# Layer B of a hybrid encoder: two contraction steps per token tile, and four query blocks' scores in one piece

## The chip, the cores and the metric

The kernel runs on one core of one Trainium2 chip. The metric is device time in microseconds (us) of one execution, as the median of the runs; lower is better. The core's engines are TensorE (PE in the profile; PEld is its loading of weights), VectorE (DVE), ScalarE (ACT), GpSimd (POOL) and SyncE (SP), which issues most of the DMAs.

## The reference

The reference is a two-layer bidirectional encoder block on 512 tokens of 1024 values in float32: per layer an RMS norm, one combined input projection, a token mixer, a SiLU gate and an output projection with a residual add. Layer A (dilated windows) is not changed. Layer B is a neighbourhood attention on an 8 x 64 grid of tokens with 16 heads of 64:

```python
def mixer_b(hn, w_in, w_out, q_gain, k_gain, rpb):
    proj = hn @ w_in                                  # 1024 -> 4 * 1024
    q, k, v, gate = jnp.split(proj, 4, axis=-1)
    q = rms_norm(q.reshape(b, s, N_HEADS, HEAD_DIM), q_gain) * (HEAD_DIM ** -0.5)
    k = rms_norm(k.reshape(b, s, N_HEADS, HEAD_DIM), k_gain)
    v = v.reshape(b, s, N_HEADS, HEAD_DIM)
    ...
        logits = jnp.einsum('bhcqd,bhrcjd->bhcqrj', qr, kr).astype(jnp.float32) + bias
        logits = jnp.where(col_valid[:, :, None, :], logits, NEG_INF)
        p = jax.nn.softmax(logits.reshape(b, N_HEADS, n_cb, NA_COL_BLOCK, wr * NA_SLAB), axis=-1)
        ...
        out = jnp.einsum('bhcqrj,bhrcjd->bhcqd', p, vr)
    ...
    y = y * jax.nn.silu(gate)
    return y @ w_out
```

## The kernel before, in words

**Precision.** Every large product is made of three matmuls: each operand is split into a high part (`h`, float32r) and a low rest (`l`), and `mm3` adds high x high, high x low and low x high into one accumulator. Weights arrive by DMA as `wraw` (8 buffers); ScalarE casts them to `wh` (6 buffers), and VectorE or GpSimd subtracts to get `wl` (5 buffers; in layer B two of five on GpSimd). The generator `splits` does this some steps ahead of use, and `next(wsteps)` hands out the next step's pair.

**Layer B.** The 16 heads are handled in 8 turns of two heads each (`hc`, called a head below, counted from 0). In `main_b`, `project_qk` makes queries, keys and values (384 columns) for four tiles of 128 tokens: the tokens' activations `hn_h`, `hn_l` are the stationary operand, the weights are streamed. `project` loops over the 8 steps of the contraction (`KT`), and in each step over the four tiles, with three matmuls each. It has one accumulator (`acc`, 512 float32 per partition) for each tile, and the pool `ps_acc` has four. After the last step `evac` copies each tile with ScalarE into `raw` (`rawq`, `rawk` or `rawb` in the profile). Then `project_t` makes the gate (512 columns, 24 matmuls) in one accumulator of the same pool, which VectorE reads into `gt`. The next head's projection follows.

**The side work.** While `main` runs, `run` pumps a second generator, `side`, between any two groups of three matmuls. In it `side_b` transposes queries and keys of the head just projected (`tp`), splits them (`qh`, `ql`, `kh`, `kl`) and computes scores, softmax and weighting. A number that `side` yields is a delay on a modelled clock that counts matmul columns; a tuple waits for a stamp; a `guard` that `main` yields makes `side` run until that stamp is there. `scores(u)` makes the logits of two of the four query blocks for both heads (`log`, two banks of the pool `ps_side`, which has four): 12 matmuls on 64 rows each, in pairs that run side by side. `softmax` follows per head and pair of blocks: a VectorE reduction that adds the bias and takes the row's minimum (into a small tile `mn`, of which there are four), a ScalarE exponential, a VectorE reciprocal, a ScalarE scaling. Then the probabilities `p` are transposed: by VectorE and a DMA round trip in heads 0 to 5, by TensorE (`turn_p`) in heads 6 and 7. `weigh` multiplies them with the values (`o`), later.

**Order.** TensorE's order is the order of the program (`manual_schedule`). The other engines' order is planned by a scheduler; `keep_in_program_order` pins single instructions behind what was written before on that engine. `chore` drops one piece of the gate's SiLU (VectorE) at a time into the loop of `project`. Every engine instruction issued through the helper class has line 85 in the profile, matmuls have line 324 and transposes 328, so groups are told apart by their tiles.

Of the kernel before, what the change touches and what calls it, by code (L numbers as in the profile page):

```python
# [27 lines left out]
KT = 8  # L28
# [18 lines left out]
def tile_hybrid_encoder(  # L47
# [24 lines left out]
    held = [False]  # L72
# [26 lines left out]
    def sb(t, off, dims):  # L99
        return bass.AP(t.tensor, t.offset + off, [t.ap[0]] + dims)  # L100
# [13 lines left out]
    def bank(name):  # L114

        return ps_side.tile([P, 512], F32, tag="side", name=name)
# [194 lines left out]
    def steps():  # L311
        for h, l, n in splits():
            for c in range(0, h.shape[1], n):
                yield h[:, c : c + n], l[:, c : c + n]
# [5 lines left out]
    def matmul(o, l, r, share=1, **kw):  # L320

        cols = max(r.free_size() / 2.4, l.free_size() / 1.2)
        clock[0] += (cols if r.dtype == F32R else r.free_size() * 4 / 2.4 * l.free_size() / P) / share
        nc.tensor.matmul(o, l, r, **kw)  # L324
# [5 lines left out]
    def mm3(o, lh, ll, rh, rl, first, last, **kw):  # L330
        matmul(o, lh, rh, start=first, stop=False, **kw)
        matmul(o, lh, rl, start=False, stop=False, **kw)
        matmul(o, ll, rh, start=False, stop=last, **kw)

    def mm3_heads(os, lh, ll, rh, rl, last):

        for n, (l, r) in enumerate(((lh, rh), (lh, rl), (ll, rh))):
            for hd in range(2):
                hs = slice(64 * hd, 64 * hd + 64)
                matmul(os[hd], l(hs), r(hs), share=2, start=(n == 0), stop=(last and n == 2))  # L340
# [14 lines left out]
    def chore(now):  # L355

        if now and chores and next(chores[0], "end") == "end":
            chores.pop(0)
# [18 lines left out]
    def project(stat_h, stat_l, n, evac, guard, need=None, after=None):  # L377

        acc = {i: ps_acc.tile([P, 512], F32, tag="acc", name="acc") for i in range(4)}
        for k in range(KT):  # L380
            chore(1 <= k < KT - 2)
            if need:
                yield need, min(k + 1, KT - 1)
            if k == KT - 1:
                yield guard
            h, l = next(wsteps)
            for i in range(4):
                mm3(acc[i][:, :n], stat_h(k, i), stat_l(k, i), h, l, k == 0, k == KT - 1)
                if k == KT - 1:
                    evac(i, acc[i])  # L390
                yield
            if after:
                yield "xn", k
                after(k)

    def project_t(acc):

# [89 lines left out]
    wsteps = steps()  # L487
    wsteps = chain([next(wsteps)], wsteps)
# [128 lines left out]
    def project_qk(n, ns, key, hc, guard, first=False, **kw):  # L617

        box = []

        def evac(i, acc):
            if not box:
                box.append(raw_q() if key == "rawq" else part(0) if key == "rawk" else raw_b(hc, n))
                box.append(sums())
                held[0] = held[0] or (key == "rawk" and hc == 0)
            raw, ss = box
            dst, src = raw[:, i, :], acc[:, :n]
            if first:
                act.copy(dst, src)
                return  # L630
            act.activation(dst, src, AF.Copy, scale=rs_n[:, i : i + 1])
            (squares_soon if key != "raw" else squares)(raw[:, i, : ns * 64], ss, i, ns, key != "raw")

        tile_of = lambda hn: lambda k, i: hn[:, k, P * i : P * (i + 1)]
        yield from project(tile_of(hn_h), tile_of(hn_l), n, evac, guard, **kw)
        raw, ss = box
        if first:
            st["first"] = raw, ss
            stamp["first",] = clock[0]
            return  # L640
        normed(raw, ss, ns, key, hc)
# [196 lines left out]
    def normalise(pr, mn):  # L838

        vec.reciprocal(mn[:, 3:4], mn[:, 2:3])  # L840
        act.activation(pr, pr, AF.Copy, scale=mn[:, 3:4])
# [428 lines left out]
    def side_b(hc):  # L1270
# [28 lines left out]

        at = lambda a, hd, i: 448 * a + 224 * hd + 32 * i  # L1300

        def scores(u):
            lgs = [bank("log") for _ in range(2)]
            for b in (2 * u, 2 * u + 1):
                if b < 3:
                    m = lambda t_, hs: t_[hs, P * b : P * b + 256]
                else:
                    m = lambda t_, hs: sb(t_[hs], 0, [[384, 2], [1, P]])
                qs = slice(P * b, P * b + P)
                o = 256 * (b % 2)  # L1310
                mm3_heads(
                    [lg[:, o : o + 256] for lg in lgs],
                    lambda hs: qh[hs, qs], lambda hs: ql[hs, qs], lambda hs: m(kh, hs), lambda hs: m(kl, hs), True,
                )
            return [(hd, u, softmax(hd, u, lgs[hd])) for hd in range(2)]

        def softmax(hd, u, lg):
            pr = wk.tile([P, 512], F32, tag="p", name="p", bufs=PB)
            for b in (2 * u, 2 * u + 1):
                mn = wk.tile([P, 4], F32, tag="mn", name="mn", bufs=4)  # L1320
                o = 256 * (b % 2)
                if b < 3:
                    parts = ((slice(0, P), o),)
                    n, ec = 256, 0
                else:
                    parts = ((slice(0, 64), o), (slice(64, P), o + P))
                    n, ec = 128, 256
                for rows, c in parts:
                    vec.tensor_tensor_reduce(
                        out=pr[rows, o : o + n],  # L1330
                        in0=lg[rows, c : c + n],
                        in1=e[rows, hd, ec : ec + n],
                        scale=1.0,
                        scalar=3.0e38,
                        op0=ALU.add,
                        op1=ALU.min,
                        accum_out=mn[rows, 0:1],
                    )
                act.activation(
                    pr[:, o : o + n], pr[:, o : o + n], AF.Exp, bias=mn[:, 0:1], scale=-1.0, accum_out=mn[:, 2:3]  # L1340
                )
                normalise(pr[:, o : o + n], mn)
            return pr
# [29 lines left out]
                pass  # L1373
            return o

        held = []
        for u in range(2):
            held += scores(u)
            yield 1200 if u == 0 else 2400
        if far(hc):  # L1380
            turned = turner(448)
            turners.append(turned)
# [25 lines left out]
    def side():  # L1408
# [33 lines left out]
        for hc in range(NHC):  # L1442
            yield from side_b(hc)
# [94 lines left out]
```

## Time and profile before

| | |
|---|---|
| Time, median of 3 runs | 845.55 us (844.61 to 847.19) |
| Profiled execution, span from first to last instruction | 844.7 us; the page gives no other time of it |
| TensorE busy | 829.5 us (98%), 6611 matmuls |
| VectorE, ScalarE, GpSimd busy | 631.8, 508.2, 291.7 us |
| Granted TensorE clock, mean | 0.999 |
| DMA | 131.97 MB, mean 156 GB/s |

How to read it: TensorE's instructions are pipelined, so a record begins before the one before has ended, and its busy share is close to full also where it works below its peak. A row of the timeline gives start, duration, engine, line, operation, output and inputs by the program's names, shape and count; in brackets stands how long the engine stood idle before it and who released it. A row of the waits gives the total in us, the number of times and the longest.

### The profile page before, as it was taken

The page shows a single profiled execution, that of the slowest core. Times are in us where ns is not written, and L with a number is a line of the kernel's source. Part 1 is how long each engine was busy: PE and PEld are TensorE (multiplying, and loading weights), DVE is VectorE, ACT ScalarE, POOL GpSimd, SP SyncE. Part 2 cuts the span into 40 slices and gives each one's busy share as a digit, 9 for nine tenths or more (in the row PEclk, how much of TensorE's full clock was granted, in tenths as well). Part 3 has the DMA queues.
Part 4 walks back from the last instruction along what each step waited for, and adds up shares of the span by engine and source line. Part 5 has one row for each costly group of instructions (what it writes and reads, how often), then busy time and mean ns, then how long its engine had stood idle before and what let it go on. Part 6 is the DMA issues. An engine that isn't in the chain of part 4 may idle for free.

```text
span 844.7 us, 18126 instructions
## 1 busy us (share of the span) xinstructions
PE 829.5 (98%) x6611; PEld 686.0 (81%) x6611; DVE 631.8 (75%) x1653; ACT 508.2 (60%) x1066; POOL 291.7 (35%) x259
## 2 busy tenths in 40 slices
PE   9999999999999999999999999999999999999998
PEld 7877878878877878878877887789998898889786
DVE  7898997896995886896896876566668767776742
ACT  7656766846846846747747728554546664666440
POOL 5042343543533533533532514213123222322201
PEclk9999999999999999999999999999999999999999
DMA  9426766676676785785776554473265456644212
GB/s 342 141 57 170 190 155 151 141 172 195 133 172 201 158 194 167 159 205 132 162 177 167 119 186 144 150 237 111 93 192 161 132 146 180 173 135 115 85 51 100
DMA packets 56169, 131.97 MB, mean 156 GB/s; under 512 B 7184, under 2 KB 24528, under 8 KB 55952
## 3 DMA queue, kind: packets, MB, share of 16 engines
q1 hardware_dynamic: 49456, 108.39, 41.7%
q0 software_dynamic: 6048, 22.02, 15.3%
q8 instruction: 52, 0.85, 0.4%
q10 hardware_dynamic: 576, 0.41, 0.2%
q14 instruction: 37, 0.30, 0.1%
HBM read 111.73 MB, written 11.72 MB: 146 GB/s over the span
## 4 chain that ended last, share of the span: by engine, by line
PE 77%; ACT 8%; DVE 7%; DMA 4%; issue 2%; POOL 1%; SPq 0%; ACTq 0%; DVEq 0%; POOLq 0%
PE acc L324 64%; PE log L324 5%; PE o L324 4%; ACT p L85 4%; PE tp L328 3%; DMA wraw<-in_w 2%; ACT wh L85 1%; DVE wl L85 1%; DVE na L85 1%; DMA yr<-y_d 1%; ACT rawk L85 1%; DVE rawq L85 1%; DVE gt L85 1%; POOL sq L85 1%; DVE tr L85 1%
## 5 line engine op out<-in xcount | busy, mean ns | idle before, releaser
L85 POOL TENSOR_TENSOR wl<-wraw,wh 128x512 fp32r<-128x512 f32 (+1 forms) x153 | 198.5, 1298 | 434.8 <-PE acc L324 214.4
L85 ACT CAST wh<-wraw 128x512 fp32r<-128x512 f32 (+1 forms) x360 | 209.5, 593 | 194.7 <-PE acc L324 155.0
L85 DVE TENSOR_TENSOR wl<-wraw,wh 128x512 fp32r<-128x512 f32 (+1 forms) x207 | 159.3, 773 | 45.5 <-PE acc L324 33.3
L324 PE MATMUL acc<-wh,hn_h 128*128 128x384 f32 (+1 forms) x488 | 186.4, 382 | 2.7 <-DVE gt L85 1.5
L324 PE MATMUL acc<-wl,hn_h 128*128 128x384 f32 (+1 forms) x488 | 177.6, 364 | 1.7 <-DVE wl L85 1.7
L324 PE MATMUL acc<-wh,hn_l 128*128 128x384 f32 (+1 forms) x488 | 177.4, 364 | 0.0
L85 ACT ACTIVATE p<-p,mn 128x256 f32<-128x256 f32 (+2 forms) x248 | 137.7, 585 | 32.3 <-DVE mn L85 32.3
L324 PEld LDWEIGHTS acc<-wh,hn_h 128*128 128x128 f32 x488 | 92.1, 189 | 21.3 <-issue 6.8
L324 PEld LDWEIGHTS acc<-wl,hn_h 128*128 128x128 f32 x488 | 92.3, 189 | 10.0 <-DVE wl L85 2.6
L324 PEld LDWEIGHTS acc<-wh,hn_l 128*128 128x128 f32 x488 | 92.0, 189 | 9.8
L324 PE MATMUL acc<-wh,mix_h 128*128 128x512 f32 x224 | 89.1, 398 | 0.0
L324 PE MATMUL acc<-wl,mix_h 128*128 128x512 f32 x224 | 87.5, 390 | 0.0
L324 PE MATMUL acc<-wh,mix_l 128*128 128x512 f32 x224 | 87.4, 390 | 0.0
L324 PE MATMUL acc<-hn_h,wh 128*128 128x512 f32 x192 | 79.0, 412 | 0.3 <-ACT rawb L85 0.2
L324 PE MATMUL acc<-hn_h,wl 128*128 128x512 f32 x192 | 75.1, 391 | 0.0
L324 PE MATMUL acc<-hn_l,wh 128*128 128x512 f32 x192 | 75.0, 391 | 0.0
L85 DVE STREAM_TRANSPOSE pt<-p 128x512 f32<-128x512 f32 (+1 forms) x60 | 40.6, 687 | 23.5 <-ACT p L85 23.4
L85 DVE TENSOR_REDUCE ss<-sq 128x4 f32<-128x256 f32 (+1 forms) x96 | 46.1, 502 | 11.8 <-POOL sq L85 5.9
L324 PE MATMUL acc<-y_h,wh 128*128 128x512 f32 x128 | 51.9, 405 | 0.5 <-ACT gt L85 0.5
L324 PEld LDWEIGHTS acc<-wh,mix_h 128*128 128x128 f32 x224 | 42.0, 188 | 9.9 <-issue 1.6
L324 PE MATMUL acc<-y_h,wl 128*128 128x512 f32 x128 | 50.0, 391 | 0.0
L324 PE MATMUL acc<-y_l,wh 128*128 128x512 f32 x128 | 50.0, 390 | 0.0
(148 smaller groups left out, 1358.9 us busy)
## 6 DMA issues: line engine op xcount, KB each, us to landing
wraw<-in_w SPq DMA_DIRECT2D x95, 512.0 KB
wraw<-in_w POOLq DMA_DIRECT2D x42, 512.0 KB, 6.9
wraw<-in_w SPq DMA_DIRECT2D x38, 384.0 KB
pt<-pt SPq DMA_DIRECT2D x106, 64.0 KB
td<-tr SPq DMA_DIRECT2D x24, 224.0 KB
pt<-td SPq DMA_DIRECT2D x24, 224.0 KB
e<-l_d SPq DMA_DIRECT2D x32, 112.0 KB
e<-l_d SPq DMA_DIRECT2D x16, 128.0 KB
```

The costliest lines, as they stand in the source:

```text
L85: m = f(*args, **kw)
L324: nc.tensor.matmul(o, l, r, **kw)
L328: nc.tensor.transpose(o, i, ident)
```

## The change

In `project`, calls without `need` and `after` (those of layer B) take two steps of the contraction at a time: two pairs of weights are drawn together, and each token tile gets its six matmuls in a row before the next tile's. The guard is yielded before the pair that holds the last step, and the pieces of `chore` fall at the start and in the middle of a pair. In `side_b`, `scores` makes all four query blocks' logits in one piece, with four banks, and only then starts the four softmaxes; the delays of 1200 and 2400 after the halves become one of 3600.

```diff
     def project(stat_h, stat_l, n, evac, guard, need=None, after=None):
 
         acc = {i: ps_acc.tile([P, 512], F32, tag="acc", name="acc") for i in range(4)}
-        for k in range(KT):
-            chore(1 <= k < KT - 2)
+        both = 1 if need or after else 2
+        for k0 in range(0, KT, both):
+            ks = range(k0, k0 + both)
+            chore(1 <= k0 < KT - 2)
             if need:
-                yield need, min(k + 1, KT - 1)
-            if k == KT - 1:
+                yield need, min(k0 + 1, KT - 1)
+            if KT - 1 in ks:
                 yield guard
-            h, l = next(wsteps)
+            ws = [next(wsteps) for _ in ks]
             for i in range(4):
-                mm3(acc[i][:, :n], stat_h(k, i), stat_l(k, i), h, l, k == 0, k == KT - 1)
-                if k == KT - 1:
-                    evac(i, acc[i])
-                yield
+                for k, (h, l) in zip(ks, ws):
+                    mm3(acc[i][:, :n], stat_h(k, i), stat_l(k, i), h, l, k == 0, k == KT - 1)
+                    if k == KT - 1:
+                        evac(i, acc[i])
+                    yield
+                if i == 1 and both == 2:
+                    chore(1 <= k0 < KT - 2)
             if after:
-                yield "xn", k
-                after(k)
+                yield "xn", k0
+                after(k0)
...
-        def scores(u):
-            lgs = [bank("log") for _ in range(2)]
-            for b in (2 * u, 2 * u + 1):
+        def scores():
+            both = [[bank("log") for _ in range(2)] for u in range(2)]
+            for b in range(4):
+                lgs = both[b // 2]
                 if b < 3:
                     m = lambda t_, hs: t_[hs, P * b : P * b + 256]
...
-            return [(hd, u, softmax(hd, u, lgs[hd])) for hd in range(2)]
+            return [(hd, u, softmax(hd, u, both[u][hd])) for u in range(2) for hd in range(2)]
...
-        held = []
-        for u in range(2):
-            held += scores(u)
-            yield 1200 if u == 0 else 2400
+        held = scores()
+        yield 3600
```

## The prediction

> **What bounds the kernel now.** I read the page first (busy shares, the chain that ended last), then the busy times by stretch for the second layer, then who TensorE waits for, and last the order of instructions on each engine over one head.
>
> ```profile
> PE 829.5 (98%) x6611; PEld 686.0 (81%) x6611; DVE 631.8 (75%) x1653; ACT 508.2 (60%) x1066; POOL 291.7 (35%) x259
> ...
> PE acc L324 64%; PE log L324 5%; PE o L324 4%; ACT p L85 4%; PE tp L328 3%; DMA wraw<-in_w 2%; ACT wh L85 1%; DVE wl L85 1%; DVE na L85 1%; DMA yr<-y_d 1%; ACT rawk L85 1%; DVE rawq L85 1%; DVE gt L85 1%; POOL sq L85 1%; DVE tr L85 1%
> ```
>
> TensorE is the bound: 829.5 of 844.7 us. One head of layer B (heads counted from 0) takes 28.2 us in the stretch of head 4 (columns: the stretch, its length, then busy time and instructions of PE, PEld, DVE, ACT and POOL, granted clock, DMA share, GB/s):
>
> ```profile
> 673.10:701.30 28.20, 27.82 (x178) 24.56 (x177) 20.29 (x66) 16.21 (x43) 8.06 (x10) 1.00 0.54 156
> ```
>
> No engine beside TensorE is over 72% of a head, the clock is at full speed, the DMA engines are half idle. So only two things can move the time: TensorE's own price per instruction, and the short stops in its stream. The steady price, by the distance of two starts (columns: start, duration, engine, what, tiles, shape):
>
> ```profile
> 649.90 0.33 PE L324 MATMUL acc<-wh,hn_h 128*128 128x384 f32 x1
> 650.07 0.33 PE L324 MATMUL acc<-wl,hn_h 128*128 128x384 f32 x1
> ...
> 666.29 0.39 PE L324 MATMUL acc<-hn_h,wl 128*128 128x512 f32 x1
> 666.51 0.39 PE L324 MATMUL acc<-hn_h,wh 128*128 128x512 f32 x1
> ```
>
> A 384-column matmul takes 0.174 us (the mean over such a run of starts; two stamps alone round to 0.17), a 512-column one 0.227. The duration of a record (0.33, 0.39) is longer because matmuls overlap, so stops are read from starts. Three matmuls make one contraction step of one token tile (0.52 us), twelve one step of four tiles (2.09 us), and eight steps one projection.
>
> **The change, part by part.** No matmul, copy, cast or DMA is added or removed. TensorE gets another order, and with it the moments at which accumulators and weight buffers come free.
>
> *Six matmuls in a row on one accumulator.* Do they cost more than three? The 512-column rows above are 24 in a row on one accumulator and cost 0.227 = 512 columns at 2.4 per ns plus 0.014; the 384-column rows, which change the accumulator every third matmul, cost 0.174 = 160 ns plus 0.014. The same overhead, so I take nothing either way.
>
> *The fourth token tile at the head's start.* The projection has four accumulators; the fourth is the one that the gate projection just before it used, and VectorE must read that into `gt` first.
>
> ```profile
> 645.04 0.33 PE L324 MATMUL acc<-wh,hn_h 128*128 128x384 f32 x1
> ...
> 646.45 0.34 PE L324 MATMUL acc<-wh,hn_l 128*128 128x384 f32 x1
> 647.16 0.45 PE L324 MATMUL acc<-wh,hn_h 128*128 128x384 f32 x1 [0.37 <-DVE gt L85]
> 647.45 0.34 PE L324 MATMUL acc<-wl,hn_h 128*128 128x384 f32 x1
> ...
> 758.99 0.34 PE L324 MATMUL acc<-wh,hn_l 128*128 128x384 f32 x1
> ...
> 759.88 0.34 PE L324 MATMUL acc<-wl,hn_h 128*128 128x384 f32 x1
> ```
> ```profile
> 646.42 0.68 DVE L85 TENSOR_TENSOR gt<-acc,rs_half 128x512 f32<-128x512 f32 x1
> ```
> ```profile
> PE acc L324 <- DVE gt L85: 1.5, 5, 0.4
> PE tp L328 <- ACT p L85: 0.8, 1, 0.8
> ```
>
> From 646.45 to 647.45 are two intervals, 0.35 without a stop; they take 1.00, so the stop and the refill behind it cost 0.65. It happens five times (the wait view counts 5), heads 3 to 7, the last costing 0.89 - 0.35 = 0.54; the five sum to 2.9 us. VectorE is done with `gt` 2.06 us after the projection's start (647.10 against 645.04). The fourth tile was due at 9 x 0.174 = 1.57; with six matmuls per tile it is due at 18 x 0.174 = 3.13. The cover is 1.07 us. What follows takes up to 0.7 of it (TensorE comes earlier, VectorE's chain does not), so it still holds. I take all 2.9; the ends are 0 and 2.9.
>
> *The first accumulator at the head's end.* The gate projection needs a free accumulator, that of token tile 0, which ScalarE copies out.
>
> ```profile
> 585.25 0.33 PE L324 MATMUL acc<-wh,hn_l 128*128 128x384 f32 x1
> ...
> 585.65 0.40 PE L324 MATMUL acc<-hn_l,wh 128*128 128x512 f32 x1
> ...
> 611.47 0.34 PE L324 MATMUL acc<-wh,hn_l 128*128 128x384 f32 x1
> ...
> 612.16 0.39 PE L324 MATMUL acc<-hn_l,wh 128*128 128x512 f32 x1
> ...
> 665.73 0.50 PE L324 MATMUL acc<-hn_h,wh 128*128 128x512 f32 x1
> ...
> 749.68 0.34 PE L324 MATMUL acc<-wh,hn_l 128*128 128x384 f32 x1
> ...
> 750.38 0.40 PE L324 MATMUL acc<-hn_l,wh 128*128 128x512 f32 x1
> ```
>
> Head 0 passes in 0.40, which is 0.174 + 0.227 with no stop: the switch itself is free. In heads 1 to 6 it takes 0.69 to 0.84; the six stops sum to 1.9 us. ScalarE, in order (p is a block of the softmax, rawk the copy of a projection's tile), and VectorE's fifth reduction:
>
> ```profile
> 660.21 0.51 ACT L85 ACTIVATE p<-p,mn 128x256 f32<-128x256 f32 x1 [2.39 <-DVE mn L85]
> ...
> 662.60 1.70 ACT L85 ACTIVATE p<-p,mn 128x256 f32<-128x256 f32 x4
> 664.20 0.50 ACT L85 CAST wh<-wraw 128x384 fp32r<-128x384 f32 x1
> ...
> 665.11 0.56 ACT L85 ACTIVATE rawk<-acc,rs_n 128x384 f32<-128x384 f32 x1
> ```
> ```profile
> 663.20 0.42 DVE L85 CUSTOM_DVE_ANT_0 p<-log,eb 128x256 f32<-128x256 f32 x1 [0.31 <-ACT p L85]
> ```
>
> The gate projection of that head began 0.19 us late at 665.73, so tile 0's last matmul began ten intervals before the unstopped 665.54, at 663.8, and ended by 664.14; its copy began 0.97 later, behind softmax work and a cast. With pairs tile 0 ends 18 matmuls, not 9, before the projection's end, 1.57 us earlier. With the same lag of 0.97 and 0.56 of copying the accumulator is free 1.4 us ahead of its use, so I take all 1.9. The other end is a loss: the copy gets no earlier (first rival) or later (second). The four copies stay the same four and only spread out.
>
> *Scores in one piece.* Each half, twelve matmuls on half the rows (six records of two), stands between 128-row matmuls:
>
> ```profile
> 658.46 0.34 PE L324 MATMUL acc<-wh,hn_l 128*128 128x384 f32 x1
> 658.73 0.39 PE L324 MATMUL log<-kh,qh 64*128 64x256 f32 x2
> ...
> 659.07 0.29 PE L324 MATMUL log<-kh,ql 64*128 64x256 f32 x2
> ...
> 659.42 0.28 PE L324 MATMUL log<-kh,ql 64*128 64x256 f32 x2
> 659.63 0.44 PE L324 MATMUL acc<-wh,hn_h 128*128 128x384 f32 x1
> 659.92 0.34 PE L324 MATMUL acc<-wl,hn_h 128*128 128x384 f32 x1
> ...
> 662.31 0.44 PE L324 MATMUL acc<-wh,hn_h 128*128 128x384 f32 x1
> ```
>
> From 659.07 to 659.42 three records take 0.35, so 0.117 each. From 658.46 to 659.92 it is 1.46; two 384-column intervals (0.35) and six records (0.70) leave 0.41 for going in and out. One piece pays it once: 0.41 a head, 8 x 0.41 = 3.3 us. The four score banks are needed at once; the last one to come free, that of the transposed keys, is given up by the same VectorE subtraction that writes kl, which the scores wait for anyhow. The second half's logits are ready at 659.63 + 0.70 = 660.3 in place of 662.3, but no softmax goes faster by it: the fifth reduction (663.20) waits for ScalarE to release the first of four small mn tiles, not for TensorE. The delays 1200 + 2400 become 3600, so the transposes behind the softmax keep their place. In head 6, which transposes on TensorE, the stop on ScalarE's p (0.8 us in the wait view) ends by ScalarE's clock, and the 0.41 won there comes back as a longer stop. So I take 7 x 0.41 = 2.9.
>
> *Weights in pairs.* Both steps' wh and wl must be there 0.52 us into a pair, and buffers come free near its end. The tightest case is the low part of the sixth step (five wl buffers): free 3.65 us into the first pair, needed 0.52 into the third, at 8.9: 5.2 us, where it was four steps, 8.3 us. The work behind a release, and the longest queue ahead of it on POOL:
>
> ```profile
> 650.86 0.56 DVE L85 TENSOR_TENSOR wl<-wraw,wh 128x384 fp32r<-128x384 f32 x1
> ```
> ```profile
> 647.92 1.19 POOL L85 TENSOR_TENSOR wl<-wraw,wh 128x384 fp32r<-128x384 f32 x1 [2.83 <-PE acc L324]
> ...
> 666.73 2.40 POOL L85 TENSOR_TENSOR sq<-rawk 128x256 f32<-128x256 f32 x4
> ...
> 672.13 1.41 POOL L85 TENSOR_TENSOR y_l<-gt,y_h 128x512 fp32r<-128x512 f32 x1 [3.01 <-ACT y_h L85]
> ```
>
> 1.19 alone, 5.0 behind both others, which do not fall together: hidden, cost 0. Without that cover each miss is a stop of TensorE (third rival). Queued behind a waiting wl are sq and y_l on POOL, reductions and `gt` on VectorE; behind a waiting cast on ScalarE, the copies and the softmax. On SP nothing is added: one load holds the two steps of a pair, so it is issued at most at the pair's start. The SiLU pieces of `gt` move from steps 1 and 2 to step 2 and its middle, on VectorE, a head before their product is used: 0. The guard for the keys moves from before the eighth to before the seventh step; the scores, which follow those keys, already start in the sixth step (658.73 in a projection begun at 645.04): 0.
>
> *Sum:* 2.9 + 1.9 + 2.9 = 7.7 us. The profiled execution spans 844.7 us, 0.85 under the median of the runs, and no other time of it is given; 844.7 becomes 837.0, and with the same 0.85 around it the median becomes 837.9 us.
>
> **The rivals.** *First: ScalarE keeps its order.* If tile 0's copy stays 6.4 us behind the first scores (665.11 against 658.73), behind the same normalising and the cast, it ends where it did, and the gate projection waits for it however early TensorE comes: heads 1 to 6 keep their 1.9, and the 0.41 won before each of these six gates is waited away. Left are 2.9 and the 0.4 of the last head, 3.3: 842.2 us. For it: ScalarE works without a hole from 660.21 past 665. Against it: the copy is ready 1.57 us earlier, and in these rows a copy already goes ahead of softmax blocks that were emitted sooner.
>
> *Second: the copies are queued behind the pair's casts.* Drawing two steps together emits two casts ahead of the last pair's copies, and the second needs a buffer that is free only at the pair's end. If it stands ahead of tile 0's copy in ScalarE's queue, the copy comes 0.17 + 0.41 (664.20 to 664.61) + 0.46 = 1.04 after the projection; with 0.1 of refill and a little hand-over 1.2 us in six heads, 7.2 in place of 1.9. The sum is then 7.7 - 1.9 - 5.3 = 0.5: 845.0 us, the same. Against it: of ScalarE's waits before casts, the row below, those that I read stand where no copy was ready. [...]
>
> ```profile
> ACT wh L85 <- PE acc L324: 47.5, 43, 4.4
> ```
>
> *Third, slower: the weights come late.* It decides where cast and subtraction take over 5.2 us from a release. A miss of 1 us in two pairs of eight heads is 16 us, less the 7.7: 853.9 us. For it: buffers are the only reserve, and POOL's subtraction already starts on a release by TensorE. Against it: 1.2 us of work in 5.2.
>
> *Fourth: better,* head 6's stop goes too: another 0.4 + 0.8, 836.7 us.
>
> **How the numbers follow.** Forecast 0.55 (837.9), first rival 0.22, fourth 0.05, second 0.10, third 0.08. The range takes in the first three: from 836.7 less 0.9 for the runs' scatter (844.61 is 0.9 under its median) and a little, 835.4, to 842.2 plus 0.6 of scatter, 842.8. The bound of 0.3% is 2.5 us, about what these runs can tell (844.61 to 847.19): faster 0.81 (forecast, first, fourth, less a hundredth), same 0.11, slower 0.08.
>
> **What would show it.** Right: no wait of TensorE for `gt` at a head's fourth tile; 0.40 between the last 384-column matmul and the second of the gate projection; one record group of scores a head with a single 0.41; heads of about 26.9 us in place of 28.2 (0.6 + 0.3 + 0.4 less); TensorE's busy time smaller by the bridged refills. Wrong: waits of TensorE for ScalarE's rawk or rawb at the gate (first or second rival, told apart by what ScalarE ran just before), or new waits for wl or wh inside a projection (third).

## The result, and the profile after

The changed kernel takes 837.23 us (median of 5 runs, 835.80 to 837.90), the kernel before 844.61 us beside it (5 runs, 843.29 to 847.19): ratio 0.9907, 95% interval 0.9894 to 0.992, or 7.4 us less. The profiled execution of the changed kernel took 836.45 us and spans 834.7.

The busy line and the chain that ended last, from the page of the changed kernel:

```profile
PE 821.2 (98%) x6611; PEld 685.0 (82%) x6611; DVE 631.2 (76%) x1653; ACT 506.6 (61%) x1066; POOL 292.9 (35%) x259
...
PE acc L324 72%; PE log L324 5%; PE o L324 5%; PE tp L328 4%; DVE wl L85 1%; DMA wraw<-in_w 1%; DMA yr<-y_d 1%; DVE rawq L85 1%; ACT wh L85 1%; DMA pt<-in_xt 1%; ACT p L85 0%; ACT rawk L85 0%; DVE ss L85 0%; DVE mixed L85 0%; ACT sq L85 0%
```

The same 6611 matmuls, TensorE busy for 8.3 us less, and TensorE's projections carry 72% of the chain where they carried 64%: the entries for `gt`, `na` and ScalarE's p are gone from it or shrunk. Head 4, from one projection's start to the next (columns as before):

```profile
668.02:694.85 26.83, 26.83 (x177) 24.63 (x176) 20.08 (x66) 16.09 (x44) 8.01 (x10) 1.00 0.57 163
```

26.83 us in place of 28.20, and TensorE busy without a hole. The waits of TensorE in all of layer B:

```profile
PE tp L328 <- ACT p L85: 1.1, 2, 0.8
```

Neither `gt` nor a copy is left in this list; only head 6's transposes wait for ScalarE. The scores of head 3, the end of its projection, and the tenth matmul of head 4's, in TensorE's timeline:

```profile
653.93 0.34 PE L324 MATMUL acc<-wh,hn_l 128*128 128x384 f32 x1
654.20 0.39 PE L324 MATMUL log<-kh,qh 64*128 64x256 f32 x2
...
655.62 0.28 PE L324 MATMUL log<-kh,ql 64*128 64x256 f32 x2
655.83 0.44 PE L324 MATMUL acc<-wh,hn_h 128*128 128x384 f32 x1
656.11 0.34 PE L324 MATMUL acc<-wl,hn_h 128*128 128x384 f32 x1
...
660.45 0.33 PE L324 MATMUL acc<-wh,hn_l 128*128 128x384 f32 x1
660.62 0.39 PE L324 MATMUL acc<-hn_h,wh 128*128 128x512 f32 x1
660.85 0.40 PE L324 MATMUL acc<-hn_l,wh 128*128 128x512 f32 x1
...
669.43 0.33 PE L324 MATMUL acc<-wh,hn_l 128*128 128x384 f32 x1
669.61 0.33 PE L324 MATMUL acc<-wh,hn_h 128*128 128x384 f32 x1
```

The scores stand in one group: 653.93 to 656.11 is 2.18, less two intervals (0.35) and twelve records (1.41) leaves 0.42 for going in and out, once. From the last 384-column matmul to the second of the gate projection it is 0.40, no stop. And the tenth matmul of head 4's projection, which before waited for `gt`, follows the ninth in 0.18.

To set the executions side by side, layer B alone is measured from its first 384-column matmul to the end of the span (rows of before and after):

```profile
567.69 0.33 PE L324 MATMUL acc<-wh,hn_h 128*128 128x384 f32 x1
```
```profile
565.19 0.33 PE L324 MATMUL acc<-wh,hn_h 128*128 128x384 f32 x1
```

Before 844.7 - 567.69 = 277.0, after 834.7 - 565.19 = 269.5: 7.5 us less. The other 2.5 us between the two spans lie in layer A, where every engine has the same instructions in the same order; in the other profiled executions below it ended between 564.2 and 566.4, so the execution profiled before was a slow one there. "Layer B" below is this length, read from the one profiled execution of each kernel.

### The profile page after: what moved, and what is told of

Read it like the earlier page. It is cut to its first block, busy times and chain, and to the rows that moved or that the text cites. A ratio compares the mean times of both kernels' runs of the same rounds, so it can differ in the third digit from the quotient of the medians.

```text
span 834.7 us, 18138 instructions
## 1 busy us (share of the span) xinstructions
PE 821.2 (98%) x6611; PEld 685.0 (82%) x6611; DVE 631.2 (76%) x1653; ACT 506.6 (61%) x1066; POOL 292.9 (35%) x259
## 4 chain that ended last, share of the span: by engine, by line
PE 87%; DVE 4%; ACT 4%; DMA 3%; issue 1%; SPq 0%; DVEq 0%; ACTq 0%
PE acc L324 72%; PE log L324 5%; PE o L324 5%; PE tp L328 4%; DVE wl L85 1%; DMA wraw<-in_w 1%; DMA yr<-y_d 1%; DVE rawq L85 1%; ACT wh L85 1%; DMA pt<-in_xt 1%; ACT p L85 0%; ACT rawk L85 0%; DVE ss L85 0%; DVE mixed L85 0%; ACT sq L85 0%
## 5 line engine op out<-in xcount | busy, mean ns | idle before, releaser
L85 DVE TENSOR_TENSOR wl<-wraw,wh 128x512 fp32r<-128x512 f32 (+1 forms) x207 | 161.5, 783 | 39.0 <-PE acc L324 22.6
L324 PE MATMUL acc<-wh,hn_h 128*128 128x384 f32 (+1 forms) x488 | 184.4, 378 | 1.2 <-DVE rawq L85 1.2
```

What stands on the lines that cost most here:

```text
L85: m = f(*args, **kw)
```

## The experiments

Every time is a median of 4 to 12 runs, and the ratio stands against the kernel before on the same chip.

**The two parts, each alone.** Scores in one piece, projection as before (against the changed kernel, shortened; the loop's body goes back with it):

```diff
-        both = 1 if need or after else 2
-        for k0 in range(0, KT, both):
-            ks = range(k0, k0 + both)
+        for k in range(KT):
...
```

> The kernel before, with only the four blocks' scores in one piece. Stops theory (three separate stops: 2.9 us for gt at the fourth tile, 1.9 us for the copy at the gate, 0.41 us a head for entering and leaving the scores): the entry price is paid once a head, but both other stops hang on ScalarE's and VectorE's work after the scores and grow by what TensorE saves in heads 1 to 6; between 0.4 and 2.9 us less than before (844.2 to 841.7), TensorE still waits for gt and for a rawk or rawb copy. Rival (the merge alone clears the stops, because softmax starts sooner): about 838, no wait for gt.

Measured: 845.18 us, ratio 1.0008 (0.9993 to 1.0022), layer B 278.0. No gain at all; the forecast's own size for the part is missed. TensorE's waits, and ScalarE and TensorE in head 3:

```profile
PE acc L324 <- ACT rawk L85: 3.8, 5, 0.8
PE acc L324 <- ACT rawb L85: 1.4, 2, 0.8
PE acc L324 <- DVE gt L85: 1.2, 5, 0.3
```
```profile
656.81 0.39 PE L324 MATMUL log<-kh,qh 64*128 64x256 f32 x2
...
663.05 0.34 PE L324 MATMUL acc<-wh,hn_l 128*128 128x384 f32 x1
664.20 0.50 PE L324 MATMUL acc<-hn_h,wh 128*128 128x512 f32 x1 [0.81 <-ACT rawk L85]
```
```profile
663.59 1.49 ACT L85 ACTIVATE rawk<-acc,rs_n 128x384 f32<-128x384 f32 x3
```

The copy of tile 0 starts 6.78 us after the first scores (656.81 to 663.59; before it was 6.38). TensorE reaches the gate earlier and waits there: 663.05 to 664.20, 0.97 of it a stop where 0.19 to 0.32 stood. Seven gate stops, 5.2 us of waiting, have eaten the 8 x 0.41. This is the first rival's mechanism, at work as soon as the pairs are not there.

The pairs alone, scores in two halves (against the changed kernel, shortened; `scores` takes its half `u` again):

```diff
-        held = scores()
-        yield 3600
+        held = []
+        for u in range(2):
+            held += scores(u)
+            yield 1200 if u == 0 else 2400
...
```

> The kernel before, with only the pairs of contraction steps. Stops theory: 4.8 us less than before (839.8), no wait of TensorE for gt or for a copy at the gate, and each half of the scores still costs 0.41 us beside its twelve matmuls. Rival (the merge clears the stops, pairs do nothing): as before, 844 to 845, with the five waits for gt.

Measured: 840.20 us, ratio 0.9948 (0.993 to 0.9966), layer B 272.5, 4.5 less. No stop for `gt` or at the gate is left; each half of the scores still pays its 0.41. So 2.9 + 1.9 is the pairs' part, less 0.25 in one new place: 

```profile
577.52 0.34 PE L324 MATMUL acc<-wh,hn_l 128*128 128x384 f32 x1
577.93 1.02 PE L324 MATMUL pk<-one,ssq 128*128 128x1 f32 x8
```

(the changed kernel at the start of layer B: 0.41 from the projection to the row sums where 0.17 would do). In every kernel here whose first steps go in a pair it is 0.41 or more, in all the others 0.17.

**Which pair does what.** First only steps 1 and 2 together, then only steps 7 and 8, with scores in halves. Below is the loop of the first, against the changed kernel and shortened; in the second the steps are cut at `(0, 1, 2, 3, 4, 5, 6, 8)`. Both also drop the piece of `chore` in the middle of a pair.

```diff
-        both = 1 if need or after else 2
-        for k0 in range(0, KT, both):
-            ks = range(k0, k0 + both)
+        cut = range(KT + 1) if need or after else (0, 2, 3, 4, 5, 6, 7, 8)
+        for k0, k1 in zip(cut, cut[1:]):
+            ks = range(k0, k1)
...
```

> The kernel before, with only steps 1 and 2 of each layer B projection taken as a pair, the other six steps singly. Stops theory: the wait for gt goes, the one at the gate stays or grows: 2.9 us less than before less up to 0.5 (841.7 to 842.2). Rival (every pair of steps gains its share, by six matmuls in a row on one accumulator): a quarter of 4.8, 843.4, with waits for gt as before.

Measured: 842.12 us, ratio 0.9968 (0.9956 to 0.998), layer B 274.2, 2.8 less: the `gt` term as forecast, and the gate's stops stay.

> The kernel before, with only steps 7 and 8 taken as a pair. Stops theory: the stop at the gate goes (1.9 us), but TensorE then comes 0.3 us earlier to the fourth tile, and VectorE's gt does not: the five waits for gt grow from 0.3 to about 0.6 us; 0.4 to 1.9 us less than before (844.2 to 842.7). Rival (every pair gains its share): 843.4, waits for gt as long as before.

Measured: 840.95 us, ratio 0.9959 (0.9945 to 0.9974), layer B 273.4, 3.6 less. That is a miss: besides the gate's stops, four of the five `gt` stops are gone as well. Head 4's projection shows it (TensorE, then VectorE):

```profile
669.94 0.33 PE L324 MATMUL acc<-wh,hn_h 128*128 128x384 f32 x1
...
671.53 0.42 PE L324 MATMUL acc<-wh,hn_h 128*128 128x384 f32 x1
```
```profile
669.23 0.78 DVE L85 TENSOR_TENSOR na<-rs 128x16 f32<-128x16 f32 x1
...
670.77 0.68 DVE L85 TENSOR_TENSOR gt<-acc,rs_half 128x512 f32<-128x512 f32 x1
```

VectorE's `gt` starts 0.83 after the projection, and is just in time for a fourth tile that is still due at 1.57. In heads 4 to 7 that start is 1.28 to 1.38 in the kernel before and in the one with only the first pair. It is 0.82 to 0.86 in the changed kernel, in the one with later transposes below, in the pairs alone, and in the three with the last pair alone and `y_l` on GpSimd. The last pair doesn't bring it everywhere: with the scores in four pieces (below) it is 1.28 to 1.30 again, with all low parts on GpSimd 1.62. The two parts of the pairs overlap, 2.8 + 3.6 against 4.5.

**What makes `gt` late.** Ahead of it stands a tiny operation on 128x16 that takes 0.17 us elsewhere and 0.78 here. In the kernel before it is this one:

```profile
672.33 1.26 DVE L85 TENSOR_TENSOR na<-rs 128x16 f32<-128x16 f32 x1
```

It ends at 673.59; GpSimd's `y_l`, shown before (672.13 and 1.41), ends at 673.54. In the kernel with the last pair the two ends are 670.01 and, by this row of GpSimd, 669.98; in the changed kernel 668.30 and 668.26:

```profile
668.57 1.41 POOL L85 TENSOR_TENSOR y_l<-gt,y_h 128x512 fp32r<-128x512 f32 x1 [2.58 <-ACT y_h L85]
```
```profile
667.49 0.81 DVE L85 TENSOR_SCALAR nv<-ss 128x16 f32<-128x16 f32 x1
```
```profile
666.93 1.33 POOL L85 TENSOR_TENSOR y_l<-gt,y_h 128x512 fp32r<-128x512 f32 x1 [1.93 <-ACT y_h L85]
```

So VectorE seemed to be held until GpSimd was done. The test takes the kernel before and moves that one subtraction:

```diff
-        (vec if last else pol).tensor_sub(l, gt, h.bitcast(F32))
+        vec.tensor_sub(l, gt, h.bitcast(F32))
```

> The kernel before, with one thing changed: in heads 0 to 6 of layer B the subtraction that writes y_l (128x512) is done by VectorE instead of GpSimd. It asks what makes gt late at the fourth tile. Theory (VectorE is held: in the kernel before the small head-norm operation ahead of gt takes 1.26 us instead of 0.17 and ends 0.05 after GpSimd's y_l ends; VectorE's own y_l takes some 0.7 there): the 1.26 is gone, gt starts 0.6 to 0.95 us after a projection's start in heads 4 to 7 where it was 1.28 to 1.38, and all or nearly all of the five gt stops are gone although the projection takes single steps: 1.7 to 2.9 us less, layer B 274.1 to 275.3, time 841.7 to 843; the gate's stops stay. Rival (gt is late because VectorE's queue is long behind the late copies, and more work on it makes it later): gt starts at 1.3 or later, its stops stay or grow, 844.5 to 848.

Measured: 841.38 us, ratio 0.9964 (0.995 to 0.9977), layer B 274.0, 3.0 less, with every `gt` stop gone although VectorE has more to do:

```profile
669.57 0.16 DVE L85 TENSOR_TENSOR na<-rs 128x16 f32<-128x16 f32 x1
669.65 0.67 DVE L85 TENSOR_TENSOR y_l<-gt,y_h 128x512 fp32r<-128x512 f32 x1
...
670.75 0.69 DVE L85 TENSOR_TENSOR gt<-acc,rs_half 128x512 f32<-128x512 f32 x1
```

The projection starts at 670.41, so `gt` starts 0.34 after it (0.25 to 0.34 in heads 4 to 7), better than expected: the planner also puts it ahead of more of the head norms. That the hold made `gt` late in the kernel before is shown, as far as one can with an order that moved by some places. It is not the only thing that does: with the scores in four pieces the hold ends right at head 4's projection's start, and `gt` is as late as before, behind a transposition and five small operations. Why the last pair alone moved `gt` forward isn't settled: its hold ended 0.07 after the projection's start, where it was 0.41, and four small operations stood behind it in place of five.

**Is the first pair needed?** Last pair and scores in one piece:

> Only the last two steps of each layer-B projection go in a pair (the first six steps go one by one, four tiles each), and the scores come in one piece. The question is whether the first three pairs do anything once the last one is there. Theory (all of it is the last pair: it brings tile 0's copy early, the early copies bring the head norms and with them gt early on VectorE, and the merge saves 0.41 a head since no copy is waited for at the gate): the one gt stop that the last pair alone left (head 3) goes too or stays at 0.6; layer B some 269.5 to 270.5 us, time 837 to 838.5. Rival (the merge, which leaves TensorE 0.4 earlier and starts four softmaxes before the copies, makes VectorE's gt late against a fourth tile that is due at 1.57 us, so that the first pair is needed): gt stops of 0.4 to 0.9 in three to six heads, layer B 271.5 to 273, time 839 to 840.5.

Measured: 838.62 us, ratio 0.9935 (0.9916 to 0.9954), layer B 271.2: between the two. Heads 4 to 7 have no stop, heads 2 and 3 have 0.32 and 0.95:

```profile
642.99 0.45 PE L324 MATMUL acc<-wh,hn_h 128*128 128x384 f32 x1 [0.78 <-DVE gt L85]
```

In head 3 of the changed kernel `gt` also starts late, 1.79 after the projection, and is done at 2.47; the first pair's due time of 3.13 covers it with 0.66 left. So, once the last pair is there, the stops of these two heads, some 1.3 us, are most of the 1.7 us between the two kernels; a refill of 0.1 in each of the other four makes up the rest. The run takes out the two middle pairs as well, but its stops all stand at the fourth tile of the first steps.

**The price of a 64-row group.** The changed kernel with the scores in four pieces:

```diff
+                if b < 3:
+                    yield 400
...
-        held = scores()
+        held = yield from scores()
```

> The changed kernel, with the scores cut into four pieces, one per query block, with some projection matmuls between them. Price theory (0.41 us for each time that TensorE goes to 64-row matmuls and back): three more pieces in seven heads, 7 x 3 x 0.41 = 8.6 us more than the changed kernel's 837.2, so 845.8; in head 6 it is hidden in the stop before the transposes. Rival (the 0.41 is a wait of the first scores for their operands, paid once a head however they are cut): 837 to 838.

Measured: 845.12 us, ratio 1.001 (0.9998 to 1.0022), layer B 277.7, 8.2 more than the changed kernel. One of the pieces:

```profile
658.68 0.34 PE L324 MATMUL acc<-wh,hn_l 128*128 128x384 f32 x1
658.95 0.39 PE L324 MATMUL log<-kh,qh 64*128 64x256 f32 x2
...
659.29 0.29 PE L324 MATMUL log<-kh,ql 64*128 64x256 f32 x2
...
659.79 0.33 PE L324 MATMUL acc<-wl,hn_h 128*128 128x384 f32 x1
```

658.68 to 659.79 is 1.11, less 0.35 and three records (0.35) leaves 0.41. The price is one per group, not one per matmul. (With three more pieces in all eight heads it would be 9.8 us more; head 6's stop, gone in this run, gives 1.6 back.)

**Head 6's stop.** The changed kernel with the transposes of head 6 later:

```diff
-        yield 3600
+        yield 6600 if hc == NHC - 2 else 3600
```

> The changed kernel, with the transposes of head 6's probabilities 3000 ns later on the modelled clock. Theory (two stops, 0.4 and 1.1 us, in which TensorE waits for ScalarE's softmax while projection matmuls are left to do): both go, 837.2 - 1.5 = 835.7. Rival (the work behind the transposes is the bound: the weighting and the last output projection come later by as much): same, 837.2, with a new wait in the output projection.

Measured: 835.31 us, ratio 0.9895 (0.9877 to 0.9913), layer B 267.9, 1.6 less than the changed kernel; TensorE's list of waits in layer B is empty. The same edit on the kernel with the last pair and one piece of scores:

> The same kernel with the delay before the transposes of head 6 raised from 3600 to 6600 on the modelled clock, as it was done to the changed kernel, where it took out the only stop left (1.2 us and its refill) and 1.6 us of time. Theory (stops of TensorE add up when they hang on different engines): 1.5 less than the kernel with the last pair and the merge, 835.5 to 837. Rival (with another order of copies and softmaxes head 6's stop stands elsewhere or a gt stop at head 7 takes it over): less than 0.7 gained.

Measured: 837.58 us, ratio 0.9921 (0.9904 to 0.9939), layer B 269.7, 1.5 less than without the edit (by the medians 1.0): the stops add up. With `y_l` on VectorE as well:

> Last pair alone, scores in one piece, later transposes in head 6, and y_l on VectorE. Left to win in that kernel were the gt stops of heads 2 and 3 (0.32 and 0.95). In head 3 the same hold is there (a 128x16 operation of 1.19 us that ends with GpSimd's y_l), in head 2 none was seen ahead of gt. Theory (the hold): head 3's stop shrinks by 0.4 to 0.95, head 2's 0.32 stays: layer B 268.8 to 269.3 instead of 269.7, time 836.6 to 837.2. Rival (queue length): both stay or grow, 837.5 to 839.

Measured: 835.87 us, ratio 0.9899 (0.9885 to 0.9912), layer B 268.3: 1.4 less, more than expected. Head 3's stop is gone and head 2's 0.31 stays. This and the changed kernel with later transposes are the two best, and their intervals overlap.

**More small tiles for the row minima.** One tile for two blocks, so that the fifth reduction needn't wait for ScalarE:

```diff
+            mns = wk.tile([P, 8], F32, tag="mn", name="mn", bufs=4)
...
-                mn = wk.tile([P, 4], F32, tag="mn", name="mn", bufs=4)
+                mn = mns[:, 4 * (b % 2) : 4 * (b % 2) + 4]
```

> The changed kernel, with room for eight minima in place of four, so that the second half's reductions need not wait for ScalarE to release the first. Theory (the earlier logits are of no use, ScalarE's order decides): the fifth reduction of a head starts about 1.5 us sooner, the time stays within 0.3% of 837.2, and the stop of head 6 shrinks by at most 0.4 us. Rival (softmax blocks that are ready sooner go ahead of tile 0's copy on ScalarE, which ends only 0.5 us before the gate projection needs it): waits for rawk or rawb come back, 1 to 3 us more.

Measured: 837.51 us, ratio 0.9913 (0.99 to 0.9926), layer B 270.1, 0.6 more than the changed kernel; the two times lie within their scatter. In the changed kernel the fifth reduction waited for ScalarE as the prediction said (first row, VectorE); now it goes at once (second row), more softmax work stands ahead of the copy on ScalarE, and a gate stop of 0.25 is back in five heads (last rows), while head 6's is gone:

```profile
658.20 0.42 DVE L85 CUSTOM_DVE_ANT_0 p<-log,eb 128x256 f32<-128x256 f32 x1 [0.24 <-ACT p L85]
```
```profile
657.66 0.41 DVE L85 CUSTOM_DVE_ANT_0 p<-log,eb 128x256 f32<-128x256 f32 x1
```
```profile
661.25 0.56 ACT L85 ACTIVATE rawk<-acc,rs_n 128x384 f32<-128x384 f32 x1
```
```profile
661.44 0.34 PE L324 MATMUL acc<-wh,hn_l 128*128 128x384 f32 x1
661.86 0.50 PE L324 MATMUL acc<-hn_h,wh 128*128 128x512 f32 x1
```

ScalarE got softmax work earlier, and the copy on which TensorE hangs came later: 6.06 us after the first scores, in the changed kernel 5.49.

**Weights made late.** All low parts of layer B's weights, and of layer A's output projection, on GpSimd:

```diff
-            pool[0] = [0, 1] if first < 16 else [1, 2] if at < mixed_jobs else [2, 5]
+            pool[0] = [0, 1] if first < 16 else [1, 2] if at < mixed_jobs else [1, 1]
```

> The changed kernel, with all low parts of layer B's weights made on GpSimd (1.0 to 1.2 us each) and none on VectorE (0.55 to 0.7). Theory (5.2 us between a buffer's release and its next use cover it): no wait of TensorE for wl inside a projection, 837.2 within 0.3%. Rival (pairs leave too little time for the weights): a wait for wl in most pairs, 0.5 to 1 us each, 32 pairs: 850 or more.

Measured: 840.94 us, ratio 0.9949 (0.9936 to 0.9963), layer B 273.8, 4.3 more than the changed kernel. No projection waits for a weight, so the third rival falls even with GpSimd doing all of them. The loss is elsewhere: 3.1 us at the start of layer B, where TensorE waits for VectorE's row sums (the last section shows it), and 1.2 behind a late `gt` in heads 2 and 3.

Three or four steps per tile weren't tried, nor were the first and the last pair without the two between.

## Why the prediction was right, and where its steps were off

The time, 837.23 us, lies 0.7 under the 837.9 forecast, and layer B lost 7.5 where the sum said 7.7. By steps:

- *The fourth tile, 2.9:* right in size; all five stops are gone, and the first pair alone brings 2.8. The cover was given as 1.07 less up to 0.7. In heads 4 to 7 more is left, since `gt` also came earlier; in head 3 it is 0.66. The step took VectorE's time of `gt` as given. It wasn't: GpSimd's `y_l` held VectorE, which the prediction had quoted as a queue for the weights only, and one moved subtraction brings as much, 3.0 of layer B, in the kernel before.
- *Six matmuls in a row on one accumulator, 0:* right, but the two equal overheads don't show it: the 2.4 columns per ns can only be worked out from the same two rows (128 columns more in 0.053 us). The changed kernel shows it, with 19 intervals of 0.173 us from 669.61 to 672.90; in the kernel before, 654.00 to 655.91 is 11 of 0.174.
- *The gate, 1.9:* right in sign and size, but the margin was mis-sized. The step said that the copy keeps its lag of 0.97 and leaves the accumulator free 1.4 us ahead. Here is the copy of the changed kernel:

```profile
659.69 0.56 ACT L85 ACTIVATE rawk<-acc,rs_n 128x384 f32<-128x384 f32 x1
```

It ends at 660.25, and the gate projection uses the accumulator at 660.62: some 0.4 us ahead. Tile 0's last matmul starts 18 intervals before 660.45, at 657.33, and ends by 657.66, so the lag was 2.0 and not 0.97 (with the pairs alone 1.5): tile 0 is done earlier, but ScalarE is still at softmax blocks and a cast until 659.69. It starts 5.49 after the first scores (654.20), so it came 0.9 nearer to them, not 1.57. In the run with more minima tiles it starts 6.06 after them, and that used up the margin.
- *Scores in one piece, 2.9:* right as part of the whole (layer B 272.5 with the pairs alone, 269.5 with both: 3.0), and its price per group is shown by the run in four pieces. But it holds only behind the pairs; alone the merge brings nothing. The sum was written as if its terms were independent, and the first rival, put at 842.2, named the mechanism that makes them dependent.
- *Head 6:* right. Its stop now has 0.84 and 0.26 of waiting, and ends 11.09 us after the first scores of that head (772.61 against 761.52); before it was 11.08 (782.20 against 771.12). The pace of ScalarE's softmax sets it, and the 0.41 won there is lost.

```profile
771.33 0.44 PE L328 MATMUL tp<-ident,p 128*128 128x128 f32 x2 [0.26 <-ACT p L85]
772.61 0.33 PE L328 MATMUL tp<-ident,p 128*128 128x128 f32 x1 [0.84 <-ACT p L85]
```

- *Weights in pairs, 0:* right but for the 0.25 at the row sums, in all kernels with a first pair. 2.9 + 1.9 + 2.9 - 0.25 = 7.45, beside the measured 7.5.
- *From span to time:* the 0.85 was wrong. Time less span is 836.45 - 834.7 = 1.75 here and 1.76 to 2.09 in the profiled executions of the experiments, so by an estimate the execution profiled before took 846.4 to 846.8, above the median. Since the 7.7 was taken off the median, nothing came of it.
- *The rivals:* the second (copies behind the pair's casts) and the third do not appear. The fourth did not happen by itself, but a later delay brings it, 1.6 us.

## What to carry to other kernels

Ask of each stop not only who released it, but what held the releaser: here TensorE waited for VectorE, which was held by one subtraction on GpSimd, and moving that was worth as much (3.0 us) as the reordering's gain at the fourth tile (2.8). Savings on a saturated engine add up only if the next wait doesn't hang on the thing that was moved: a copy that keeps its distance to the scores gives back what the scores saved (ratio 1.0008 for the scores alone), so measure each part alone and together. A group of matmuls on part of the rows costs its entry and exit once, 0.41 us here, so such groups are best kept whole.

## What the runs showed of the hardware

**Some of VectorE's operations were held while GpSimd subtracted:** 0.78 to 1.26 us for a tiny one that takes some 0.17 elsewhere. Besides the three pairs of ends above, the run with all low parts on GpSimd shows it on larger operations (VectorE, then GpSimd; the second VectorE row is the changed kernel):

```profile
574.60 4.84 DVE L85 TENSOR_TENSOR ssq<-ssq,sqx 128x512 f32<-128x512 f32 x4 [1.10 <-ACT sqx L85]
```
```profile
574.72 3.07 DVE L85 TENSOR_TENSOR ssq<-ssq,sqx 128x512 f32<-128x512 f32 x4
```
```profile
573.33 2.29 POOL L85 TENSOR_TENSOR wl<-wraw,wh 128x384 fp32r<-128x384 f32 x2 [1.97 <-PE acc L324]
577.49 2.81 POOL L85 TENSOR_TENSOR wl<-wraw,wh 128x512 fp32r<-128x512 f32 x2 [1.87 <-PE acc L324]
```

Four additions took 4.84 us instead of 3.07, and the row sums behind them were late. Not every operation waited. In the changed kernel a transposition started inside the `y_l` that holds `nv` (666.93 to 668.26) and took as long as the one at 666.06, outside it:

```profile
666.99 0.61 DVE L85 STREAM_TRANSPOSE tr<-p 128x384 f32<-128x384 f32 x1
```

In the three pairs above VectorE's operation, `na` twice and `nv` once, ended 0.03 to 0.05 us after GpSimd's subtraction, so it was held to that one's end. What sets these operations apart from the transposition was not shown.

**TensorE's granted clock was halved behind a short stop.** Behind that wait, in the profiled execution of the same run (the timeline of TensorE, then a stretch with columns as in the head's row above; the granted clock follows POOL):

```profile
577.68 0.34 PE L324 MATMUL acc<-wh,hn_l 128*128 128x384 f32 x1
579.59 1.02 PE L324 MATMUL pk<-one,ssq 128*128 128x1 f32 x8 [1.57 <-DVE ssq L85]
580.48 0.42 PE L324 MATMUL acc<-wh,hn_h 128*128 128x384 f32 x1
```

```profile
581.00:584.20 3.20, 3.20 (x12) 3.20 (x11) 1.49 (x11) 0.58 (x1) 0.61 (x1) 0.50 0.11 42
```

TensorE was idle for 1.57 us, then did eight one-column matmuls, and some 3.2 us of projection ran at a granted clock of 0.50: ten matmuls start there, where 18 fit at 0.174. About 1.6 us are lost behind a wait of 1.6. Between the last matmul of the projection (577.68) and the next (580.48) lie 2.8 us with little work in them. It is one stop in one execution, and what set the slow clock off can't be told from it.
